# Encoder block on one core: one tile for w_out and feed-forward operands in the place of the normalised input, output tiles split a group ahead, another order of the attention's deferred work

## The chip, the core and the metric

The kernel runs on 1 core of one Trainium2 chip. The metric is the device time in microseconds (us) of one execution. A kernel's figure is the median of several executions. "PE" is the matrix engine, "DVE" the vector engine, "ACT" the scalar engine, "POOL" the general engine and "SP" the engine whose queue issues nearly all DMA transfers. Each engine works through its own list in order. A wait at the head of a list holds up everything behind it.

## What is computed

One block of a transformer encoder for 1024 tokens of width 1024, all in float32. The reference, cut to what matters:

```python
h = layer_norm(x, ln0_g, ln0_b)
proj = h @ w_in + b_in                      # 1024 x (3*512 + 512 + 2*128 + 2*1024)
qa, ka, va, qb, kb, vb, ga, gb = split(proj)
# na: 8 heads, each token sees 8 x 16 neighbours on a 16 x 64 grid, bias rpb
y_na  = neighbourhood_attention(qa, ka, va, rpb) @ w_branch_na
# swa: 8 query heads over 2 key/value heads, |i-j| <= 128, a sink logit
y_swa = windowed_gqa_with_sink(rotary(qb), rotary(kb), vb, sink) @ w_branch_swa
mixed = sigmoid(ga) * y_na + sigmoid(gb) * y_swa
h = layer_norm(2**0.25 * h + mixed @ w_out + b_out, ln1_g, ln1_b)
u = square(relu(h @ w_ff1 + b_ff1))         # 1024 x 4096
return layer_norm(2**0.25 * h + u @ w_ff2 + b_ff2, ln2_g, ln2_b)
```

## The kernel before

**Products.** Float32 factors are split into two fp16 parts, a high and a low one, and three fp16 products stand for one float32 product. A 128x512 piece of result so takes 12 or 24 matmuls of one kind. A split is one ACT instruction (the high part) and one DVE instruction (scaled value minus high part); before it stands a scale, for which ACT sums squares, PE adds the sums over the partitions (a 128x2 matmul on ones), and DVE and POOL finish. The gate products and both feed-forward products use a 2x2 block scheme with fewer products (Winograd's form of Strassen's), whose operands are sums of blocks: A11, A12, A21, A22 and S1 to S4.

**Stages, in the order of time.** First layer norm and the first projections (to 100 us in the trace); attention, while PE fills the gaps with projection matmuls (100 to 400); the rest of the gate products (to 476); the branch products with w_branch and the gates (to 563); w_out with the second layer norm (to 657); the first feed-forward product (657 to 950); the second, with the last layer norm (to the end).

**The order of work is written by hand**: Python code issues the instructions in one sequence, and each engine's list is what falls to it. What matters around the change:

- `steps(s, n)` is one attention step for one pair of query blocks, with n "fill" matmuls (L430), 12 in the steps to 240 us and 18 after. In it, `part_a` issues the scores of step s+2 (L780, L781, two PSUM banks, `ps_s` and `ps_t`). DVE reads them with bias and row maximum (L782), ACT takes the exponentials (L801, L804), `part_l` makes the low part of the probabilities on DVE (L813) and SP transposes them with a DMA into `pt` (L816). `part_c` multiplies by the values (L888, bank `ps_o`, two buffers), and two steps share one bank. ACT takes the upper half out (`evac`, L894), and DVE adds the lower half later (`evac2`, L897), which frees the bank.
- `defer(count, fn, ...)` puts a piece of work off until so many fill matmuls have been issued, and `flush` runs what is due. A step has flushes in the middle and one at its end; only the one at the end runs the pieces that need PE. D_E2 is the count of `evac2`. `norm` (L859) scales the finished chunk by the reciprocals of its sums, which DVE makes (L832, L834), PE transposes (L838, into `ps_t`) and SP brings back through DRAM (L851).
- Other work passes through the same lists: the gathering of projections (ACT L620, L700), the rotary shuffle (DVE L628), the query's high part (ACT L677) and low part (DVE L682), the low halves of weight chunks (DVE L266), and sums for scales (PE L194 into `ps_s`, DVE L200).
- In the branch stage `wo_load`, `wo_square`, `wo_split` prepare the eight 128-row pieces of w_out. The raw rows go through a ring of two buffers "raw"; the split ones lie in `wo`, in the place (pool `r1`) that the normalised input `hT` held until the gate products ended. `between` is work put between the matmuls of a product. `o_hi` and `o_lo` (L1280, L1287) split the attention's output for the branch.
- In the w_out stage, group g is 128 tokens: `split_mx(g)` (L1503, L1504) splits the mixed input, `out_mm(g, half)` (L1628) is 24 matmuls, then `ln1_norm`, `turn` (eight transposes, L1656), `turn_evac` (L1664, L1667) and `combine` (L1673, L1686 to L1690: block sums and their splits). The first feed-forward weights ("head", p = 0 to 3) are prepared here too: `head_w` loads, `squares1` (ACT L1705) and `sum_sq1` (PE L1710), `scale1`, `head_split` (L1719, L1722).
- The first feed-forward product follows (`ff1_mm`, L1795). At its start, A22 is split whole by `comb_hi` (ACT L2025) and `comb_lo` (DVE L2028).

Of the kernel before, what the change touches and what calls it, by code (L numbers as in the profile page):

```python
# [16 lines left out]
P = 128  # L17
D = 1024
# [58 lines left out]
D_E2 = 12  # L77
# [16 lines left out]
def encoder_block(ctx, tc, x, w_in, w_br, w_out, w_ff1, w_ff2, par, rows, rpbp,  # L94
# [10 lines left out]
    r1x, wx = ExitStack(), ExitStack()  # L105
    r1p = r1x.enter_context(tc.tile_pool(name="r1p", bufs=1))
# [330 lines left out]
    def defer(*fns, pe=False, early=False, only=False):  # L437

        later.append([fns[0], fns[1:], pe, early or only, only])
# [414 lines left out]
    def norm(o_chunk):  # L854
        rb = recip.pop(o_chunk)
        sc = na_v[o_chunk][1][:, 1:2] if o_chunk < 4 else swa_sc[0][:, o_chunk // 2 - 2:o_chunk // 2 - 1]
        for x in range(2):
# [4 lines left out]
    def part_c(s):  # L862
# [26 lines left out]
        if t % 2 == 1:  # L889
# [47 lines left out]
    with tc.manual_schedule(engines=MANUAL):  # L937
# [110 lines left out]
        def steps(s, n, before_b=None, before_c=None):  # L1048
# [17 lines left out]
            flush(False)  # L1066
# [5 lines left out]
            flush(False)  # L1072
            pump(part[2])
            flush()
# [318 lines left out]
        def wo_load(k):  # L1393
            raw = wo_raw[k] = wp.tile([P, D], F32, tag="raw", name="raw", bufs=2)
# [39 lines left out]
        for n, (p, i) in enumerate(gseq[2:], 2):  # L1434
# [13 lines left out]
            if n in (4, 5, 6, 7, 10, 11):  # L1448
# [15 lines left out]
        wo = r1p.tile([P, 2, NK, D], F16, tag="r1", name="wo")  # L1464
# [10 lines left out]
        mhl = {}  # L1475
# [23 lines left out]
        def split_mx(g):  # L1499

            m = xps[g % 2].tile([P, 2, 8, P], F16, tag="m", name="m")
# [37 lines left out]
        for f in range(8):  # L1539
            for half in range(2):  # L1540
                if half == 0:
                    wo_split(f)
                    if f + 3 < 8:
# [3 lines left out]
                else:  # L1547
                    if f + 2 < 8:
                        wo_load(f + 2)
                    if f and f + 1 < 8:  # L1550
                        b_split(f + 1)
# [123 lines left out]
    def combine(g):  # L1675
# [15 lines left out]
        split_op("S1", s1, ts_)  # L1691

# [119 lines left out]
    with tc.manual_schedule(engines=MANUAL):  # L1812
# [10 lines left out]
        for g in range(NCG):  # L1823
            out_mm(g, 0, 0, 8)
            if 2 <= g + 1 < NCG:
                split_mx(g + 1)
# [10 lines left out]
            if g == 7:  # L1837
# [4 lines left out]
            if g == 7:  # L1842
                for p in range(2, 4):
                    scale1(p, head_ps[p])
                more_ring(0)
# [7 lines left out]
            if 2 <= g < 4:  # L1853
# [7 lines left out]
            if g == 6:  # L1861
                for p in range(2, 4):
                    squares1(p, raws[p])
# [12 lines left out]
            if g < 2:  # L1876
# [4 lines left out]
            if g == 5:  # L1881
                for p in range(2, 4):
                    head_w(p)
# [63 lines left out]
        r1x.close()  # L1947
        qp = ctx.enter_context(tc.tile_pool(name="qp", bufs=1, reuse_waits="tile"))
        for i, n in enumerate(("S3", "S4", "A22")):
            t = places[n] = qp.tile([P, 8192], F16, tag=f"q{i}", name="h" + n)  # L1950
            ops[n] = t[:, 0:4096].rearrange("p (a k n) -> p a k n", a=2, k=4)
        usl = qp.tile([P, 8, 512], F32, tag="q3", name="usl")
        ufree = [usl[:, i] for i in range(8)]
# [614 lines left out]
```

## Times and profile before

| what | us |
| --- | --- |
| median of 3 executions | 1257.42 (1257.39 to 1257.99) |
| the profiled execution, its own time | 1256.27 |
| its span in the trace | 1254.5 |
| PE busy | 1216.4, 97% of the span |
| DVE busy | 971.1, 77% |
| ACT busy | 868.5, 69% |
| POOL busy | 330.5, 26% |

Read the busy shares first: PE is busy nearly throughout, so the time is its work and the gaps in it. The mean granted clock of PE is 0.994. Which stage holds the gaps, and who ends them, is read in the stretches by stage and in the list of PE's waits, which the prediction shows.

### The profile page before, as it was taken

The page shows a single profiled execution, that of the slowest core. Times are in us where ns is not written, and L with a number is a line of the kernel's source. Part 1 is how long each engine was busy: PE and PEld are TensorE (multiplying, and loading weights), DVE is VectorE, ACT ScalarE, POOL GpSimd, SP SyncE. Part 2 cuts the span into 40 slices and gives each one's busy share as a digit, 9 for nine tenths or more (in the row PEclk, how much of TensorE's full clock was granted, in tenths as well). Part 3 has the DMA queues.
Part 4 walks back from the last instruction along what each step waited for, and adds up shares of the span by engine and source line. Part 5 has one row for each costly group of instructions (what it writes and reads, how often), then busy time and mean ns, then how long its engine had stood idle before and what let it go on. Part 6 is the DMA issues. An engine that isn't in the chain of part 4 may idle for free.

```text
span 1254.5 us, 17213 instructions
## 1 busy us (share of the span) xinstructions
PE 1216.4 (97%) x6070; PEld 607.8 (48%) x6070; DVE 971.1 (77%) x1418; ACT 868.5 (69%) x1415; POOL 330.5 (26%) x368
## 2 busy tenths in 40 slices
PE   7999889999999999999999999999999999999996
PEld 4545556555555444444444444444444444444443
DVE  7687888788787985645678977778857777898888
ACT  6567779998895667853567877787776746344446
POOL 5212220443430003446620013422300002211207
PEclk9999999999999999999999999999999999999998
DMA  8654657767764446636233357766637535363333
GB/s 312 198 183 87 153 127 166 169 170 169 161 162 104 151 151 201 202 101 251 101 151 109 133 191 248 246 234 233 215 108 264 218 135 226 126 260 126 126 109 134
DMA packets 177879, 216.84 MB, mean 173 GB/s; under 512 B 111745, under 2 KB 125313, under 8 KB 171137
## 3 DMA queue, kind: packets, MB, share of 16 engines
q1 hardware_dynamic: 176816, 214.89, 54.0%
q8 instruction: 47, 0.77, 0.3%
q10 hardware_dynamic: 976, 0.87, 0.2%
q14 instruction: 40, 0.32, 0.1%
HBM read 130.69 MB, written 59.33 MB: 151 GB/s over the span
## 4 chain that ended last, share of the span: by engine, by line
PE 71%; DVE 11%; ACT 8%; issue 3%; POOL 3%; DMA 1%; SPq 0%; POOLq 0%; DVEq 0%; ACTq 0%
PE ps_mm L430 13%; PE ps_t L1795 6%; PE ps_o L1795 6%; PE ps_s L2273 6%; PE ps_mm L2273 6%; PE ps_mm L1795 6%; PE ps_t L2273 5%; PE ps_o L2273 5%; PE ps_s L1795 2%; PE ps_o L888 2%; PE ps_o L1176 2%; PE ps_mm L1176 1%; PE ps_t L1176 1%; ACT ss L801 1%; PE ps_o L420 1%
## 5 line engine op out<-in xcount | busy, mean ns | idle before, releaser
L430 PE MATMUL ps_mm<-hT 128*128 128x512 f16 x960 | 227.5, 381 | 5.2 <-DVE hT L399 2.0
L1795 PEld LDWEIGHTS <-tw 128*128 128x128 f16 x1248 | 122.1, 99 | 146.1 <-issue 1.6
L2273 PEld LDWEIGHTS <-hS 128*128 128x128 f16 x1008 | 98.7, 98 | 118.2
L430 PEld LDWEIGHTS <-hT 128*128 128x128 f16 x960 | 90.7, 99 | 103.6 <-issue 14.3
L801 ACT ACTIVATE ss<-ss,sk 128x384 f32<-128x384 f32 (+1 forms) x128 | 73.9, 578 | 32.7 <-DVE sk L782 32.1
L1795 PE MATMUL ps_t<-hS,tw 128*128 128x512 f16 x384 | 88.1, 379 | 1.5 <-ACT sn L1899 1.1
L430 PE MATMUL ps_mm<-hT,wpair 128*128 128x512 f16 x288 | 70.0, 384 | 1.1 <-ACT hT L700 1.1
L1989 DVE TENSOR_TENSOR usl<-usl 128x512 f32<-128x512 f32 x64 | 52.3, 818 | 23.5 <-ACT usl L1917 23.3
L201 POOL TENSOR_TENSOR hT<-hT 128x2 f32<-128x2 f32 x30 | 29.7, 989 | 150.9 <-DVE hT L200 150.9
L1716 POOL TENSOR_TENSOR c<-c 128x2 f32<-128x2 f32 x16 | 15.5, 975 | 195.0 <-DVE c L1715 195.0
L2293 POOL TENSOR_TENSOR acc<-acc,rst 128x512 f32<-128x512 f32 x16 | 31.8, 1987 | 122.5 <-DMA rst<-xr_d 114.6
L2106 DVE SCALAR_TENSOR_TENSOR hS<-stg,c,hS 128x2048 f16<-128x2048 f32 x21 | 49.9, 2378 | 7.7 <-ACT hS L2103 7.7
L888 PE MATMUL ps_o<-pt,vv 128*128 128x256 f16 (+1 forms) x448 | 49.1, 250 | 5.9 <-DMA pt<-pl 3.8
L1722 DVE SCALAR_TENSOR_TENSOR tw<-raw,c,tw 128x512 f16<-128x512 f32 x60 | 51.2, 853 | 4.2 <-ACT tw L1719 3.9
L2273 PEld LDWEIGHTS <-hA 128*128 128x128 f16 x336 | 32.9, 98 | 39.7
L1176 PEld LDWEIGHTS <-hT 128*128 128x128 f16 x336 | 32.8, 99 | 39.6 <-issue 1.1
L813 DVE SCALAR_TENSOR_TENSOR pl<-ss,pl 128x768 f16<-128x768 f32 (+1 forms) x42 | 46.0, 1096 | 2.5 <-ACT pl L804 2.4
L888 PEld LDWEIGHTS <-vv 128*128 128x128 f16 x448 | 35.7, 98 | 23.0 <-issue 6.7
L1795 PE MATMUL ps_o<-hS,tw 128*128 128x512 f16 x192 | 44.0, 379 | 0.0
L1719 ACT ACTIVATE tw<-raw,c 128x512 f16<-128x512 f32 x60 | 41.7, 708 | 2.8 <-DVE raw L1760 2.8
L2273 PE MATMUL ps_mm<-hA,hS 128*128 128x512 f16 x192 | 42.9, 379 | 0.0
L2273 PE MATMUL ps_s<-hA,hS 128*128 128x512 f16 x192 | 42.7, 379 | 0.0
(435 smaller groups left out, 3045.5 us busy)
## 6 DMA issues: line engine op xcount, KB each, us to landing
us_d<-usl SPq DMA_DIRECT2D x112, 256.0 KB, 3.0
stg<-us_d SPq DMA_DIRECT2D x28, 1024.0 KB, 4.8
raw<-in_w_ff SPq DMA_DIRECT2D x24, 512.0 KB, 5.6
sg<-sg_d SPq DMA_DIRECT2D x32, 256.0 KB, 2.9
hA<-in_w_ff SPq DMA_DIRECT2D x8, 1024.0 KB, 7.8
hS<-in_w_ff SPq DMA_DIRECT2D x8, 1024.0 KB, 8.0
hT<-in_w_in SPq DMA_DIRECT2D x60, 128.0 KB, 2.5
hT<-in_w_in SPq DMA_DIRECT2D x11, 512.0 KB, 4.6
```

Of the source, the lines that this page charges most:

```text
L430: PE.matmul(ps, a[:, k, :], act(b, k), start=(k == 0 and i == 0), stop=(k == NK - 1 and i == 2))
L801: ACT.activation(p, p, AF.Exp, bias=nm[:, i:i + 1], scale=-1.0, accum_out=sums_l[o_chunk][:, hh, 2 * t + i:2 * t + i + 1])
L813: DVE.scalar_tensor_tensor(out=pl[:, n:2 * n], in0=e[:, 0:n], scalar=P_SCALE, in1=pl[:, 0:n], op0=ALU.mult, op1=ALU.subtract)
L888: PE.matmul(o, vs, move(part), start=(m == 0 and part == 0), stop=(m == len(runs) - 1 and part == 1))
L1176: PE.matmul(ps, w[:, a, k, :], act[:, b, k, :], start=(first and k == 0 and m == 0), stop=(k == 3 and m == 2), skip_group_check=True)
L1719: ACT.activation(hi_lo(slot, 0), src, AF.Copy, bias=0.0, scale=w_scale(p))
L1722: DVE.scalar_tensor_tensor(out=hi_lo(slot, 1), in0=src, scalar=w_scale(p), in1=hi_lo(slot, 0), op0=ALU.mult, op1=ALU.subtract)
L1795: PE.matmul(ps, ww, act[:, part, k, :], start=(first and k == 0 and m == 0), stop=(k == 3 and m == 2), skip_group_check=True)
L1989: DVE.tensor_tensor(out=out, in0=a, in1=b, op=op)
L2106: DVE.scalar_tensor_tensor(out=slot[:, :, 1, :], in0=src, scalar=scale, in1=slot[:, :, 0, :], op0=ALU.mult, op1=ALU.subtract)
L2273: PE.matmul(ps, st[:, a, part, j * P:(j + 1) * P], w[:, a, wpart, :], start=(first and a == 0 and m == 0), stop=(a == 3 and m == 2), skip_ ...
L2293: POOL.tensor_tensor(out=z, in0=z, in1=t, op=ALU.add)
```

## The change

- **Attention.** D_E2 goes from 12 to 14. `norm` is deferred by itself, in two halves (counts D_E2+2 and D_E2+8), and runs only in the flush in the middle of a step (`mid=True`). The flush at the end of a step is gone; the one behind `part_c` now runs everything, PE's pieces too. As the counts fall due at other flushes, DVE's `evac2`, shuffle, query low part and the reciprocals change place against L782 and L813.
- **One tile `r1w`** takes the place of the normalised input: the first half is `wo`, the second holds the raw rows of w_out from k = 2 on (which no longer share the ring of two). Later, A22, the raw weights of the heads p = 2 and 3, S3 and S4 lie in it; `usl`, the partial results of the first feed-forward product, moves to the second halves of S1 and S2.
- **Branch.** `wo_load(f+2)` is issued in the first half of f rather than the second; `o_lo(5)` comes after the last gate product; `between` (two sums for scales on PE) goes from behind the first product to the middle of the second.
- **w_out stage.** `split_mx(g+2)` at group g in place of g+1. `head_w(2)` and `(3)` at groups 2 and 3 (were at 5), their `squares1` at 4 and 5 (were both at 6), their sums and scales at 6 (were at 7). `combine` from group 4 on also splits its part of A22, and `comb_hi`, `comb_lo` of A22 go.
- **Start of the first feed-forward product.** `ff1_mm(1, 2)` and the work behind two earlier products come before `turn(7)`.

PE has the same instructions in number before and after.

```diff
-D_E2 = 12
+D_E2 = 14
...
-    def flush(pe=True, early=False):
+    def flush(pe=True, early=False, mid=False):
         for e in list(later):
-            if e[0] <= 0 and (pe or not e[2]) and (e[3] or not early) and (early or not e[4] or not in_steps):
+            if e[0] <= 0 and (pe or not e[2]) and (e[3] or not early) and (early or not e[4] or not in_steps) \
+                    and (mid or not e[5] or not in_steps):
...
                 if t == 3 and o_row == 64:
-                    defer(D_E2, evac2, 2, lambda: norm(o_chunk))
+                    defer(D_E2, evac2)
+                    for x in range(2):
+                        defer(D_E2 + 2 + 6 * x, lambda x=x: norm(o_chunk, x), mid=True)
...
-            flush(False)
+            flush(False, mid=True)
             pump(part[1])
             if before_c:
                 before_c()
             if s >= C_LAG:
                 part_c(s - C_LAG)
-            flush(False)
+            flush()
             pump(part[2])
-            flush()
...
-            raw = wo_raw[k] = wp.tile([P, D], F32, tag="raw", name="raw", bufs=2)
+            raw = wo_raw[k] = wp.tile([P, D], F32, tag="raw", name="raw", bufs=2) if k < 2 else wo_rest[:, k]
...
                 o_hi(n_o)
-                if n < 10:
+                if n < 7:
                     o_lo(n_o)
                 n_o += 1
-        o_lo(6)
-        o_lo(7)
+        for c in (5, 6, 7):
+            o_lo(c)
...
-        wo = r1p.tile([P, 2, NK, D], F16, tag="r1", name="wo")
+        r1w = r1p.tile([P, 4, NK, S], F16, tag="r1", name="r1w")
+        wo = r1w[:, 0:2]
+        wo_rest = r1w[:, 2:4].rearrange("p a k s -> p (a k s)").bitcast(F32).rearrange("p (k n) -> p k n", n=D)
...
-            m = xps[g % 2].tile([P, 2, 8, P], F16, tag="m", name="m")
+            if g < 2:
+                xm.append(xps[g].tile([P, 2, 2, 8, P], F16, tag="m", name="m"))
+            m = xm[g % 2][:, g // 2 % 2]
...
-                gemm3(ps, bws[f], lambda part, k: act(part, k, half), nk=4, k0=4 * gi)
-                if gi == 0 and between:
+                n = 2 if gi and between else 4
+                gemm3(ps, bws[f], lambda part, k: act(part, k, half), nk=n, k0=4 * gi, last=(n == 4))
+                if n == 2:
                     between()
+                    gemm3(ps, bws[f], lambda part, k: act(part, k + 2, half), nk=2, k0=6, first=False)
...
                     wo_split(f)
+                    if f + 2 < 8:
+                        wo_load(f + 2)
...
+    qs = [r1w[:, i].rearrange("p k s -> p (k s)") for i in range(4)]
+    q3 = [qs[3][:, 4096 * i:4096 * (i + 1)].bitcast(F32) for i in range(2)]
+    for i in range(2):
+        raws[2 + i] = q3[i].rearrange("p (r c k n) -> p r c k n", r=2, c=2, k=4)
+    q_place(2, "A22")
...
+        split_op("A22", a22, ts_)
...
-            if 2 <= g + 1 < NCG:
-                split_mx(g + 1)
+            if g + 2 < NCG:
+                split_mx(g + 2)
...
-            if g == 7:
+            if g == 6:
                 head_ps += [sum_sq1(p, "o") for p in range(2, 4)]
...
-            if 2 <= g < 4:
+            if 2 <= g < 6:
                 squares1(g - 2, raws[g - 2])
...
-            if g == 6:
-                for p in range(2, 4):
-                    squares1(p, raws[p])
...
-            if g < 2:
+            if g < 4:
                 head_w(g)
...
-        usl = qp.tile([P, 8, 512], F32, tag="q3", name="usl")
+        usl = [places[n][:, 4096:8192].bitcast(F32).rearrange("p (a n) -> p a n", a=4) for n in ("S1", "S2")]
...
         ff1_mm(1, 1)
+        after1(0, 1)
+        after1(0, 2)
+        ff1_mm(1, 2)
         turn(7)
         turn_evac(7)
         more_ring(1)
-        after1(0, 1)
-        after1(0, 2)
-        ff1_mm(1, 2)
         combine(7)
...
-            if n == 0:
-                comb_hi("A22")
-            elif n == 1:
-                comb_lo("A22")
-            elif n == 2:
+            if n == 2:
                 more_tw()
```

**How the lists move.** In the changed kernel the line numbers are one higher from the attention on, and some 17 higher in the w_out stage. The first place is DVE's list in the attention, at 129 to 140 us of the trace of before; L782 (L783 in the changed kernel) reads scores, `wpair` is the low half of a weight chunk, `q` the query's low part, `oT` the `evac2`. Before:

```order
L813 SCALAR_TENSOR_TENSOR pl<-ss,pl 128x640
L897 TENSOR_TENSOR oT<-ps_o,oT 64x512
L628 STREAM_SHUFFLE qs<-qf 128x512
L682 TENSOR_TENSOR q<-qf,q 64x4x16x8 x2
L782 ISA ss,sk<-ps_s,bd,snk 128x384
L782 ISA sk 128x1
L782 ISA ss,sk<-ps_t,bd,snk 128x384
L782 ISA sk 128x1
L266 SCALAR_TENSOR_TENSOR wpair<-hT,wpair 128x1024
L813 SCALAR_TENSOR_TENSOR hT<-ss,hT 128x768
```

And the changed kernel, from the same reading of scores on:

```order
L783 ISA ss,sk<-ps_s,bd,snk 128x384
L783 ISA sk 128x1
L783 ISA ss,sk<-ps_t,bd,snk 128x384
L783 ISA sk 128x1
L266 SCALAR_TENSOR_TENSOR wpair<-hT,wpair 128x1024
L814 SCALAR_TENSOR_TENSOR hT<-ss,hT 128x768
L898 TENSOR_TENSOR oT<-ps_o,oT 64x512
L629 STREAM_SHUFFLE qs<-qf 128x512
L783 ISA ss,sk<-ps_s,bd,snk 128x384
L783 ISA sk 128x1
L783 ISA ss,sk<-ps_t,bd,snk 128x256
L783 ISA sk 128x1
L814 SCALAR_TENSOR_TENSOR pl<-ss,pl 128x768
L683 TENSOR_TENSOR q<-qf,q 64x4x16x8 x2
```

`evac2` and the shuffle now stand behind the reading of the next scores and its L814, and the two query low parts one reading later still; before, all stood ahead of it. The second place is SP's list at the start of the branch stage (`sg` are gate rows, `braw` the raw rows of w_branch). Before:

```order
L1512 DMA sg<-sg_d 128x512 x6
L1373 DMA braw<-in_w_br 128x1024
L1512 DMA sg<-sg_d 128x512 x2
L1395 DMA raw<-in_w_out 128x1024
```

And the changed kernel:

```order
L1518 DMA sg<-sg_d 128x512 x6
L1397 DMA r1w<-in_w_out 128x1024
L1375 DMA braw<-in_w_br 128x1024
L1518 DMA sg<-sg_d 128x512 x4
```

The raw rows of w_out are now ahead of the raw rows of w_branch and of two gate rows. The third place is ACT's list in the w_out stage, around group 6 (`junk` is the sum of squares, `hS` and `hA` and `r1w` operands, `tw` weights). Before:

```order
L285 ACTIVATE z<-z,mv 128x1024
L1705 ACTIVATE junk,c_5477<-hS_6064 128x2048
L1705 ACTIVATE junk,c_5477<-hS_6065 128x2048
L1672 CAST hS_6065<-s2t 128x4x128
L1672 CAST hS_6064<-s1t 128x4x128
L1719 ACTIVATE tw_5476<-hA_5475,c_5477 128x512 x2
L1667 ACTIVATE mx<-ps_t,c_5477 128x128 x6
```

And the changed kernel:

```order
L285 ACTIVATE z<-z,mv 128x1024
L1688 CAST hS_6060<-s2t 128x4x128
L1688 CAST hS_6059<-s1t 128x4x128
L1688 CAST r1w<-mx 128x4x128
L1736 ACTIVATE tw_5470<-hA_5469,c_5471 128x512 x2
L1683 ACTIVATE mx<-ps_t,c_5471 128x128 x6
```

The two sums of squares of 128x2048 are gone from here (they stand one in each of the two groups before), and a cast of A22's part has come.

More of the change, by code (lines that the diff above doesn't have):

```diff
@@ L435, in encoder_block, with defer @@
     later = []
-    def defer(*fns, pe=False, early=False, only=False):
-        later.append([fns[0], fns[1:], pe, early or only, only])
-    def flush(pe=True, early=False):
+    def defer(*fns, pe=False, early=False, only=False, mid=False):
+        later.append([fns[0], fns[1:], pe, early or only, only, mid])
+    def flush(pe=True, early=False, mid=False):
         for e in list(later):
-            if e[0] <= 0 and (pe or not e[2]) and (e[3] or not early) and (early or not e[4] or not in_steps):
+            if e[0] <= 0 and (pe or not e[2]) and (e[3] or not early) and (early or not e[4] or not in_steps) \
+                    and (mid or not e[5] or not in_steps):
                 later.remove(e)
@@ L852, in load_recip, with norm @@
                               rl_d[o_chunk, hh * 8:(hh + 1) * 8, :].rearrange("a b -> (a b)").partition_broadcast(64))
-    def norm(o_chunk):
-        rb = recip.pop(o_chunk)
+    def norm(o_chunk, *xs):
+        rb = recip[o_chunk]
         sc = na_v[o_chunk][1][:, 1:2] if o_chunk < 4 else swa_sc[0][:, o_chunk // 2 - 2:o_chunk // 2 - 1]
-        for x in range(2):
+        for x in xs or range(2):
             z = oT[:, o_chunk, x * 512:(x + 1) * 512]
@@ L1546, in encoder_block @@
                         b_scale(f + 1)
[L1547 to L1551, printed above, removed]
+                elif f and f + 1 < 8:
+                    b_split(f + 1)
                 g, h = (f, 1) if half == 0 else (f + 1, 0)
@@ L1596, in encoder_block, with q_place @@
     op_places("A11", "A12")
+    qs = [r1w[:, i].rearrange("p k s -> p (k s)") for i in range(4)]
+    q3 = [qs[3][:, 4096 * i:4096 * (i + 1)].bitcast(F32) for i in range(2)]
+    for i in range(2):
+        raws[2 + i] = q3[i].rearrange("p (r c k n) -> p r c k n", r=2, c=2, k=4)
+    def q_place(i, n):
+        places[n] = qs[i]
+        ops[n] = qs[i][:, 0:4096].rearrange("p (a k n) -> p a k n", a=2, k=4)
+    q_place(2, "A22")
     tw3 = hp.tile([P, 4, 2, 512], F16, tag="t3", name="tw3")
@@ L1841, in encoder_block @@
                 head_ps = [sum_sq1(p, "o") for p in range(2)]
-            if g == 7:
+            if g == 6:
                 for p in range(2, 4):
                     scale1(p, head_ps[p])
+            if g == 7:
                 more_ring(0)
@@ L1880, in encoder_block @@
                     scale1(p, head_ps[p])
-            if g == 5:
-                for p in range(2, 4):
-                    head_w(p)
             if g == 6:
@@ L1946, in after1 @@
                 act_fn(p, 0, "A21", a, None, 0)
[L1947 to L1951, printed above, removed]
-        usl = qp.tile([P, 8, 512], F32, tag="q3", name="usl")
-        ufree = [usl[:, i] for i in range(8)]
+        for i, n in enumerate(("S3", "S4")):
+            q_place(i, n)
+        usl = [places[n][:, 4096:8192].bitcast(F32).rearrange("p (a n) -> p a n", a=4) for n in ("S1", "S2")]
+        ufree = [u[:, i] for u in usl for i in range(4)]
         ff1_mm(0, 1)
@@ L2181, in second @@
         def second(n):
-            return places[n][:, 4096:8192].bitcast(F32)
+            return q3["S1 S2".split().index(n)] if n in ("S1", "S2") else places[n][:, 4096:8192].bitcast(F32)
         def turn_over(i):
@@ L2442, in encoder_block @@
                 if n == 1 and j == 1:
-                    t = qp.tile([P, 2, 4, 512], F32, tag="q3", name="w2c")
-                    wring[0:0] = [t[:, x] for x in range(2)]
+                    wring[0:0] = usl
                     nc.sync.dma_start(xts[0][:, 0, :], row_bc(0))
```

10 lines of the change are left out of this document (5 added, 5 removed).

## The prediction

> **What bounds the kernel now.** I began with the stretches by stage, to see where PE has gaps. Columns: stretch, its length, then busy time (and instructions) of PE, PE's weight load, DVE, ACT and POOL, then the granted clock, DMA share and GB/s.
>
> ```profile
> 100.00:240.00 140.00, 128.06 (x742) 76.45 (x740) 111.59 (x231) 114.63 (x243) 38.90 (x53) 0.98 0.63 143
> 140.00:150.00 10.00, 7.60 (x38) 4.42 (x38) 8.90 (x16) 7.34 (x17) 2.82 (x4) 0.83 0.56 142
> 180.00:190.00 10.00, 8.48 (x44) 5.31 (x44) 8.89 (x19) 7.34 (x16) 1.42 (x3) 0.83 0.65 176
> 240.00:400.00 160.00, 160.00 (x919) 93.11 (x918) 131.47 (x266) 136.58 (x267) 49.89 (x65) 1.00 0.68 158
> 625.00:700.00 75.00, 69.04 (x333) 32.72 (x332) 62.37 (x95) 53.69 (x90) 13.51 (x15) 1.00 0.32 114
> 700.00:1215.00 515.00, 514.99 (x2409) 235.96 (x2408) 408.35 (x443) 334.45 (x444) 92.86 (x64) 1.00 0.55 193
> ```
>
> PE is without a gap in 240 to 400 and 700 to 1215, so nothing can be won there. It lacks 140.00 - 128.06 = 11.9 us in the first half of the attention and 75.00 - 69.04 = 6.0 us around the second layer norm. In 140:150 and 180:190 the clock is 0.83, which costs 10 x 0.17 = 1.7 us each, 3.4 together. 515 us over 2409 matmuls gives 0.214 us for one.
>
> The lists of PE's waits say who ends the gaps: total, times, longest. First 100 to 240 us.
>
> ```profile
> PE ps_o L888 <- DMA pt<-pl: 3.8, 2, 3.1
> PE ps_t L838 <- DVE sk L782: 2.2, 1, 2.2
> PE ps_mm L430 <- ACT hT L700: 2.2, 2, 1.1
> PE ps_o L888 <- DMA pt<-hT: 2.1, 1, 2.1
> PE ps_s L194 <- DVE sk L782: 1.6, 2, 1.3
> ```
>
> They add up to the 11.9. Next the branch stage (465 to 563; 2.3 in all), then 625 to 700 us (5.9).
>
> ```profile
> PE ps_mm L1176 <- DVE go L1251: 0.8, 1, 0.8
> PE ps_t L422 <- DVE wb L1391: 0.7, 1, 0.7
> PE ps_s L1491 <- DVE prm L1485: 0.6, 1, 0.6
> PE ps_s L1402 <- ACT bc L1398: 0.2, 1, 0.2
> ```
>
> ```profile
> PE ps_t L1656 <- ACT z L285: 2.0, 2, 1.6
> PE ps_o L1710 <- ACT junk L1705: 1.7, 1, 1.7
> PE ps_t L1795 <- ACT sn L1899: 1.1, 1, 1.1
> PE ps_mm L1628 <- DVE m L1504: 0.5, 1, 0.5
> PE ps_t L1795 <- DVE tw L1722: 0.4, 1, 0.4
> PE ps_s L1795 <- DVE usl L1919: 0.3, 1, 0.3
> ```
>
> PE's own work is the same before and after, so the change is worth what it takes from these 20.1 us and the 3.4 of the clock, less what it adds.
>
> **Attention.** The worst gaps have one cause, followed back in the timelines (start, duration, instruction, idle time before it and who ended it) of PE, DVE and ACT.
>
> ```profile
> 130.51 0.34 PE L781 MATMUL ps_t<-kl,q 128*128 128x384 f32 x1
> 134.31 0.28 PE L781 MATMUL ps_t<-kl,q 128*128 128x256 f32 x1
> 143.42 0.82 PE L888 MATMUL ps_o<-pt,vv 128*128 128x256 f16 x8 [2.10 <-DMA pt<-hT]
> ```
>
> ```profile
> 119.37 0.01 DVE L628 LOAD_MASK_SELECT qs<-qf  x1 [2.45 <-ACT qf L620]
> ...
> 130.58 0.68 DVE L897 TENSOR_TENSOR oT<-ps_o,oT 64x512 f32<-64x512 f32 x1
> ...
> 135.27 0.69 DVE L682 TENSOR_TENSOR q<-qf,q 64x512 fp32r<-64x512 f32 x1 [2.52 <-ACT q L677]
> 135.99 0.62 DVE L782 CUSTOM_DVE_ANT_0 ss<-ps_s,bd,snk 128x384 f32<-128x384 f32 x1
> ...
> 137.07 2.11 DVE L266 SCALAR_TENSOR_TENSOR wpair<-hT,wpair 128x1024 f16<-128x1024 f32 x1
> 139.11 0.94 DVE L813 SCALAR_TENSOR_TENSOR hT<-ss,hT 128x768 f16<-128x768 f32 x1
> ```
>
> ```profile
> 134.63 0.61 ACT L677 CAST q<-qf 64x512 fp32r<-64x512 f32 x1 [2.60 <-PE ps_t L781]
> ```
>
> The scores were done at 130.85, but DVE read them (L782) at 135.99: it stood 2.52 us at the query's low part (L682), which waits for ACT's high part, and this for PE's scores at 134.31, the last readers of the old query. L813 so ended at 140.05, and the transposed probabilities came to PE at 143.42, 3.4 us later. In the changed list L682 and the shuffle stand behind this L813. Then L782 starts at 130.9, L266 at 131.9 and L813 at 134.0, ending at 134.9, and the probabilities arrive by 138.3. PE would want them at 143.42 less the two gaps (2.1 and 1.1), so 140.2. Both gaps go. The pair around 180 us (3.1 and 1.1) has the same shape and goes with it, the 1.3 of L194 too, and L838's 2.2, whose DVE stood 2.45 us at the shuffle (119.37): of that I keep 0.8, as the reciprocals now stand behind one more L813. With both pairs the clock spells should go. Gross: 2.1 + 1.1 + 3.1 + 1.1 + 1.3 + 2.2 + 3.4 = 14.3, less 0.8 = 13.5.
>
> What it adds: `evac2` (L897) now follows the next L782, L266 and L813, and until it ends, the bank for the pair after next isn't free. From the scores that is (137.07 - 135.99) + (139.11 - 137.07) + 0.94 + 0.68 = 4.7 us. PE needs the bank one step (134.31 - 130.51 = 3.8) and eight fill matmuls (1.7) later, 5.5: a margin of 0.8. It doesn't hold where L813 is slow:
>
> ```profile
> 125.77 1.78 DVE L813 SCALAR_TENSOR_TENSOR pl<-ss,pl 128x640 f16<-128x640 f32 x1
> ...
> 188.43 0.82 DVE L813 SCALAR_TENSOR_TENSOR pl<-ss,pl 128x640 f16<-128x640 f32 x1
> ```
>
> ```profile
> 125.59 1.28 POOL L632 TENSOR_TENSOR qs<-qs,rt 128x512 f32<-128x512 f32 x1
> ```
>
> The same shape takes 1.78 while POOL runs and 0.82 otherwise, 0.96 more than a margin of 0.8. Some 8 places have the L266 in between. Bounds: 0, and 8 x 1.78 = 14.2. I take 0.5 at each, 4.0, nearer to the lower end, since the fast form leaves room. Behind a waiting L888 stand four fill matmuls and the next scores, so such a wait is paid in full. Net 9.5 (-0.7 to 13.5).
>
> The Trainium skill (SBUF — State Buffer, "Who interferes with whom") says that a DVE instruction with two SBUF inputs contends for a shared port with a GpSimd instruction that reads SBUF; the pair of L813 above agrees. By it, a new order pays wherever it lays L813 on POOL's rotary sums. It also says (TensorE: Matmul & The Clock Gate, "HAM oscillation — how this bites in real kernels") that only idle stretches over about 3.4 us bring the slow clock. The trace differs: the clock is 0.83 where the gaps were 1.1 and 2.1. By the page the two spells would come from something else and stay, and the sum below would be 11.6 in place of 15.0; by the trace it is 15.0, and a pair of waits left over costs 1.7 more.
>
> On SP the two loads of the reciprocals (L851) now stand behind one more transpose; PE doesn't read them, and `norm`, which does, is itself put off by 2 to 8 fill matmuls more. If they came late, `norm` would stop DVE ahead of the next L782, which is the stop described above, at the end of each of the eight chunks; I cost it at nothing, as the half-chunk `norm` in the middle flush stands behind that step's L813.
>
> In the steps after 240 us there is no gap to win and, with 18 fill matmuls, 6 x 0.214 = 1.3 us more room for the new order. I cost it at nothing; without that room it would be the 0.5 a pair of above.
>
> **Branch.** Two rows of ACT and DVE:
>
> ```profile
> 493.89 1.06 ACT L1398 ACTIVATE bc<-raw 128x1024 fp8e5<-128x1024 f32 x1 [1.81 <-DMA raw<-in_w_out]
> ```
>
> ```profile
> 468.37 1.22 DVE L1287 TENSOR_TENSOR oS<-oT,oS 128x1024 f16<-128x1024 f32 x1
> ```
>
> ACT waits 1.81 us for raw rows of w_out, and the 0.2 and 0.7 of PE come from ACT's list behind it. The rows are now asked for half a product pair earlier (12 matmuls or more, 2.6 us) and wait for no buffer: both go. The 0.8 goes as `o_lo(5)` (1.22) leaves the place before L1251. The 0.6 goes as `between` moves six matmuls (1.3) later. The added load order holds back two gate rows and one w_branch piece on SP, one transfer each; they were not waited for on PE. Of 2.3 I take 1.9 (0 to 2.3).
>
> **Second layer norm and start of the feed-forward.**
>
> ```profile
> 650.12 1.90 ACT L1705 ACTIVATE junk<-hS 128x2048 fp8e5<-128x2048 f32 x1
> ...
> 678.84 1.88 ACT L2025 CAST hS<-mx 128x2048 f16<-128x2048 f32 x1
> ```
>
> ```profile
> 654.69 0.69 DVE L1673 TENSOR_TENSOR hS<-s2t,hS 128x512 f16<-128x512 f32 x1 [5.15 <-ACT hS L1672]
> ...
> 686.18 2.29 DVE L2028 TENSOR_TENSOR hS<-mx,hS 128x2048 f16<-128x2048 f32 x1
> ```
>
> The two sums of squares (1.9 each) leave ACT's place ahead of the casts for which DVE stood 5.15 us; with them goes the 1.7 of L1710. The 1.6 of L1656 has 12 matmuls (2.6) of cover more and goes. The 1.1 goes because A22's 1.88 on ACT and 2.29 on DVE are done in quarters in the groups before (four times 0.69 on DVE, somewhat less on ACT), in time that DVE stood idle. The 0.3 goes with them. The 0.5 goes too, but comes back one group later at L1656, since the chain from `z` to the transposes is no shorter. The 0.4 of L1722 grows to about 1.2: PE comes there 4.1 us earlier (1.7 + 1.6 + 0.5 + 0.3), DVE only 5.15 - 1.9 = 3.3. Left are 0.4 + 0.5 + 1.2 = 2.1, more with A22's pieces in the way: I take 2.3 left of 5.9, 3.6 won (1.5 to 5.5). The head loads p = 2 and 3, moved two and three groups ahead, and `usl` and A22 in other places of the same memory wait for `wo` and S1, S2, which are read last before those are due; the DMA share of 0.32 in 625:700 leaves the loads room. Were one of them late, `squares1` would wait on ACT, and the 1.7 would stay.
>
> Sum: 9.5 + 1.9 + 3.6 = 15.0. Against the profiled execution, 1256.27 - 15.0 = 1241.3; the median stood 1257.42 - 1256.27 = 1.15 above it, so 1242.4.
>
> **The rivals.**
> - *DVE becomes the bound of the attention.* For it: 111.59 of 140 busy, and 8.90 of 10 in 140:150; once PE doesn't wait, the same DVE work falls into some 126 us, 89%, and each collision with POOL adds 0.96. Against it: DVE's own stops (2.45, 2.52) go as well. The attention then gains nothing, the rest 5.5: 1251.9, from 1248 to 1254.9.
> - *All gaps go and no new one comes.* For it: the fast L813 leaves 0.8 at each bank. 13.5 + 1.9 + 3.6 = 19.0 gives 1238.4, with all of the 2.3 and 5.9 another 2.7 less: about 1237, from 1235.7 to 1238.4.
> - *The change moves the waits, and the total stays*: the work of each engine is the same, and each removed stop returns at the next product. For it: the 0.5 does just this. Against it: L813 is followed to a margin of 140.2 - 138.3 = 1.9. About 1257.
> - *Slower: the late `evac2` holds the bank `ps_o` at every pair.* The first half has 16 pairs of steps. If each waits the 1.78 of a slow L813, 28.5 us stand against 19.0 won: 1257.42 + 9.5 = 1266.9. It is slower from 12 pairs on (21.4). Against it: only about half the steps have the L266 ahead, and POOL is busy only 38.90 of 140 us.
>
> **How the numbers follow.** Forecast (1238.4 to 1248) 0.55; DVE the bound 0.20; all gaps gone 0.10; no change 0.06; slower 0.09. A measurement of this kernel tells about 0.2% (2.5 us) from no change, so faster means under 1254.9: 0.55 + 0.20 + 0.10 = 0.85; same 0.06, slower 0.09. For 8 in 10 the range takes the forecast's own, most of the full gain and three quarters of the DVE case: 1235.5 to 1252.5.
>
> **What would show it.** Right: in 100 to 240 us PE's waits at L888 for `pt` fall to the 0.7 that stands there beside the 3.1, the clock is 1.00 in both spells, L682 has no long stop ahead of L782, and small waits at L888 on DVE's `oT` appear. In 465 to 563 almost nothing is left; at the start of the feed-forward some 2 us, at L1656 and on `tw`. Wrong: waits at L888 on `oT` of over 1 us in most pairs, DVE without idle time while PE waits for `pt`, or gaps in 240 to 400.

## The result, and the profile after

The changed kernel takes 1238.08 us (median of 4, 1237.36 to 1239.03), the kernel before 1257.7 on the same chip: a ratio of 0.9843, with a 95% interval of 0.9826 to 0.986. It is 19.6 us faster. The forecast was 1242.4, with a range of 1235.5 to 1252.5. The profiled executions took 1256.27 us (before) and 1237.68 (after), with spans of 1254.5 and 1235.7.

The stretches by stage of the kernel after (columns as in the prediction; the work in a stretch of clock time came later before, by up to 12 us in the attention and by up to 18 from 625 us on):

```profile
100.00:240.00 140.00, 135.86 (x810) 81.73 (x808) 122.02 (x252) 123.18 (x261) 42.95 (x55) 1.00 0.68 156
240.00:400.00 160.00, 159.62 (x922) 92.07 (x920) 129.75 (x258) 135.11 (x258) 51.81 (x66) 1.00 0.68 159
625.00:700.00 75.00, 72.73 (x348) 34.34 (x349) 65.08 (x103) 56.88 (x103) 4.10 (x6) 1.00 0.30 102
700.00:1215.00 515.00, 515.00 (x2409) 236.10 (x2408) 410.36 (x439) 333.75 (x447) 103.50 (x76) 1.00 0.53 189
```

PE's idle time in 100 to 240 us falls from 11.9 to 4.1 us, although DVE is now busy for 122.0 of 140 us rather than 111.6, and the clock there is 1.00. PE's waits in the kernel after, for 100 to 240 us, then 465 to 563, then 625 to 700:

```profile
PE ps_s L194 <- DVE sk L783: 1.9, 3, 0.8
PE ps_o L889 <- DMA pt<-hT: 1.5, 1, 1.5
PE ps_o L889 <- DVE oT L898: 0.7, 1, 0.7
```

```profile
PE ps_mm L1637 <- ACT m L1509: 0.9, 1, 0.9
```

```profile
PE ps_t L1672 <- ACT z L285: 1.6, 1, 1.6
PE ps_s L1812 <- DVE hS L1931: 1.3, 1, 1.3
PE ps_t L1812 <- DVE tw L1739: 0.3, 1, 0.3
```

The six waits of over 1 us in the attention are gone, and so are all four of the branch stage. New are 1.5 and 0.7 at L889, 0.9 at the first w_out product, 1.3 at L1812, and 0.4 at L430 near 361 us, in a stretch that had no gap before. The 1.6 at the transposes (L1672) is in the sixth group, where before 0.4 stood; the 1.6 of before was in the last.

To see what each stage is worth, I measure from one PE instruction to another that stands at the same place in both kernels. In PE's timeline of before these are the first scores, the first gate product, the first transposes of the second layer norm, and the last sum for a scale in the first feed-forward product:

```profile
88.92 0.47 PE L780 MATMUL ps_s<-kh,q 128*128 128x256 f32 x1
...
400.14 2.11 PE L1176 MATMUL ps_mm<-hT 128*128 128x512 f16 x9
...
581.63 1.04 PE L1656 MATMUL ps_t<-ident,z 128*128 128x128 f32 x8
...
915.19 0.28 PE L1710 MATMUL ps_s<-c 128*128 128x2 f32 x2
```

And after:

```profile
88.61 0.47 PE L781 MATMUL ps_s<-kh,q 128*128 128x256 f32 x1
...
387.78 1.46 PE L1178 MATMUL ps_mm<-hT 128*128 128x512 f16 x6
...
567.11 1.04 PE L1672 MATMUL ps_t<-ident,z 128*128 128x128 f32 x8
...
896.78 0.28 PE L1727 MATMUL ps_s<-c 128*128 128x2 f32 x2
```

| stage, us | before | after | gain | forecast |
| --- | --- | --- | --- | --- |
| attention (scores to gate products) | 311.22 | 299.17 | 12.05 | 9.5 |
| gates and branch (to the transposes) | 181.49 | 179.33 | 2.16 | 1.9 |
| w_out and first feed-forward | 333.56 | 329.67 | 3.89 | 3.6 |

The rest of the span's 18.8 us, 0.7, lies ahead of the scores and in the last 340 us. Each row rests on one trace of each kernel. How far such a length varies is seen in those kernels below whose order of work in a stage is the changed one's: the attention takes 298.3 to 300.3 us in eight traces, the w_out stage 329.65 to 329.82 in five that have no slow clock there. So the 12.05 is known to about 1 us, and the 3.89 more closely.

### The profile page after: what moved, and what is told of

Its sections match the earlier page's. It is cut to its first block, busy times and chain, and to the rows that moved or that the text cites. A ratio compares the mean times of both kernels' runs of the same rounds, so it can differ in the third digit from the quotient of the medians.

```text
span 1235.7 us, 17241 instructions
## 1 busy us (share of the span) xinstructions
PE 1210.1 (98%) x6070; PEld 606.1 (49%) x6070; DVE 976.1 (79%) x1421; ACT 867.3 (70%) x1418; POOL 333.9 (27%) x368
## 4 chain that ended last, share of the span: by engine, by line
PE 78%; DVE 8%; ACT 6%; issue 2%; POOL 2%; DMA 1%; SPq 0%; POOLq 0%; ACTq 0%; DVEq 0%
PE ps_mm L430 14%; PE ps_t L1812 6%; PE ps_o L1812 6%; PE ps_mm L1812 6%; PE ps_mm L2278 6%; PE ps_s L2278 6%; PE ps_t L2278 5%; PE ps_o L2278 5%; PE ps_s L1812 3%; PE ps_o L889 2%; PE ps_o L1178 2%; PE ps_mm L1178 1%; PE ps_t L1178 1%; PE ps_t L420 1%; PE ps_t L421 1%
## 5 line engine op out<-in xcount | busy, mean ns | idle before, releaser
L430 PE MATMUL ps_mm<-hT 128*128 128x512 f16 x960 | 226.4, 380 | 4.5 <-DVE hT L399 2.0
L1812 PEld LDWEIGHTS <-tw 128*128 128x128 f16 x1248 | 122.1, 99 | 145.0 <-DVE tw L1739 0.8
L2278 PEld LDWEIGHTS <-r1w 128*128 128x128 f16 x1008 | 98.7, 98 | 118.4
L430 PEld LDWEIGHTS <-hT 128*128 128x128 f16 x960 | 90.7, 99 | 102.0 <-issue 12.0
L430 PE MATMUL ps_mm<-hT,wpair 128*128 128x512 f16 x288 | 68.8, 380 | 0.0
L201 POOL TENSOR_TENSOR hT<-hT 128x2 f32<-128x2 f32 x30 | 25.6, 852 | 114.1 <-DVE hT L200 114.1
L2112 ACT ACTIVATE hA<-r1w,c 128x2048 f16<-128x2048 f32 x10 | 20.0, 1996 | 50.0 <-DVE r1w L2167 26.8
L2115 DVE SCALAR_TENSOR_TENSOR r1w<-stg,c,r1w 128x2048 f16<-128x2048 f32 x21 | 49.6, 2360 | 4.0 <-ACT r1w L2112 4.0
L2278 PEld LDWEIGHTS <-hS 128*128 128x128 f16 x336 | 32.9, 98 | 39.4
L889 PE MATMUL ps_o<-pt,vv 128*128 128x256 f16 (+1 forms) x448 | 49.2, 250 | 2.2 <-DMA pt<-hT 1.5
L814 DVE SCALAR_TENSOR_TENSOR pl<-ss,pl 128x768 f16<-128x768 f32 (+1 forms) x42 | 46.3, 1101 | 2.2 <-ACT pl L805 2.0
L1998 DVE TENSOR_TENSOR hS<-hS,hS 128x512 f32<-128x512 f32 x41 | 33.6, 820 | 14.6 <-ACT hS L1929 14.5
L889 PEld LDWEIGHTS <-vv 128*128 128x128 f16 x448 | 35.5, 98 | 19.3 <-DVE oT L898 1.9
L1812 PE MATMUL ps_t<-hS,tw 128*128 128x512 f16 x192 | 44.1, 379 | 0.3 <-DVE tw L1739 0.3
L1812 PE MATMUL ps_t<-r1w,tw 128*128 128x512 f16 x192 | 44.0, 379 | 0.0
L1812 PE MATMUL ps_o<-r1w,tw 128*128 128x512 f16 x192 | 44.0, 379 | 0.0
```

The costliest lines, as they stand in the source:

```text
L430: PE.matmul(ps, a[:, k, :], act(b, k), start=(k == 0 and i == 0), stop=(k == NK - 1 and i == 2))
L814: DVE.scalar_tensor_tensor(out=pl[:, n:2 * n], in0=e[:, 0:n], scalar=P_SCALE, in1=pl[:, 0:n], op0=ALU.mult, op1=ALU.subtract)
L889: PE.matmul(o, vs, move(part), start=(m == 0 and part == 0), stop=(m == len(runs) - 1 and part == 1))
L1812: PE.matmul(ps, ww, act[:, part, k, :], start=(first and k == 0 and m == 0), stop=(k == 3 and m == 2), skip_group_check=True)
L1998: DVE.tensor_tensor(out=out, in0=a, in1=b, op=op)
L2115: DVE.scalar_tensor_tensor(out=slot[:, :, 1, :], in0=src, scalar=scale, in1=slot[:, :, 0, :], op0=ALU.mult, op1=ALU.subtract)
```

## The experiments

Each kernel was timed beside the kernel before on its own chip. "Stage" below is the length between the same PE instructions as in the table, from the kernel's own trace.

**The attention's order.** Two kernels split the change in two.

```diff
 # att_undone: the changed kernel with
-D_E2 = 14
+D_E2 = 12
-                    defer(D_E2, evac2)
-                    for x in range(2):
-                        defer(D_E2 + 2 + 6 * x, lambda x=x: norm(o_chunk, x), mid=True)
+                    defer(D_E2, evac2, 2, lambda: norm(o_chunk))
-            flush(False, mid=True)
+            flush(False)
 ...
-            flush()
+            flush(False)
             pump(part[2])
+            flush()
 # att_alone: the kernel before with the reverse of this
```

> The changed kernel with the attention's part undone (D_E2 12, evac2 and norm together, the flush at the end of a step back); storage, branch and w_out stage as changed. Theory: the attention's order is worth the 12.1 us by which the traces part there (101 to 406 us), and nothing after it depends on it: 1238.1 + 12.1 = 1250.2, with the waits of before at L888 (2.1 and 3.1) and a clock of 0.83 in two stretches of 10 us. Rival (storage helps the attention too): under 1246.

> The kernel before with the attention's part of the change alone. Theory: 1257.7 - 12.1 = 1245.6, and the small waits left in 100 to 240 us are those of the changed kernel (1.5 and 0.7 at L889, 1.9 at L194). Rival (parts not additive, a wait of the attention's order returns in the gate products): over 1249.

Measured: undone, 1251.8 us (ratio 0.9944, 0.9929 to 0.9959); alone, 1244.31 (0.9889, 0.9873 to 0.9906). The product of the two ratios is 0.9834, the whole change 0.9843: the parts add up. The stage of the attention is 312.88 us without its part and 298.53 with it alone. The theory holds: the attention's gain comes without the new storage and the later stages, and goes with them in place.

**What in it does the work.** Two more kernels undo one half each.

```diff
 # de2_12: the changed kernel with
-D_E2 = 14
+D_E2 = 12
 # endflush: the changed kernel with
-            flush()
+            flush(False)
             pump(part[2])
+            flush()
```

> The changed kernel with D_E2 back at 12 and all else as changed, so that evac2 stands ahead of the reading of the scores again, but query low part and shuffle keep their new places. Theory (DVE's stop at the query's low part and the shuffle was the cause, evac2's place is not): within 2 us of the changed kernel, 1236.5 to 1240, with evac2 ending over 1 us before its bank is wanted. Rival (evac2 ahead of the scores' reading was the delay): 1242 or more, with waits at L889 for pt.

> The changed kernel with the flush for PE's pieces moved back to the end of a step (the one behind part_c runs only the others, as before), D_E2 still 14 and norm in halves. Theory: this flush is what sets shuffle and query low part ahead of or behind L783, so most of the attention's 12.1 us is lost: 1246 to 1252, with DVE idle for 2 us and more at L683 ahead of L783. Rival (D_E2 and the halves of norm carry the gain): under 1241.

With the flush at the end of the step back, the kernel takes 1249.07 us (0.9923, 0.9908 to 0.9937), 11 more than the changed one, and the stage is 310.33. DVE's and ACT's timelines of that kernel show the old stop:

```profile
136.81 0.69 DVE L683 TENSOR_TENSOR q<-qf,q 64x512 fp32r<-64x512 f32 x1 [4.15 <-ACT q L678]
137.53 0.62 DVE L783 CUSTOM_DVE_ANT_0 ss<-ps_s,bd,snk 128x384 f32<-128x384 f32 x1
```

```profile
136.17 0.61 ACT L678 CAST q<-qf 64x512 fp32r<-64x512 f32 x1 [4.22 <-PE ps_t L782]
```

DVE stands 4.15 us at the query's low part, and L783 behind it reads scores that were done by 132.4 us. The flush moves every piece that is due, not the query's work alone; that the stop at L683 is what costs is read from these rows. So the cause is the place of the query work ahead of the scores' reading, and one flush decides it.

With D_E2 at 12 the kernel takes 1236.24 us (0.9825, 0.981 to 0.984), 1.8 less than the changed one at the medians; its stage is 296.48, 2.7 shorter than in the trace of the changed kernel and 1.8 to 3.8 shorter than in the eight traces of that order. Its waits in 100 to 240 us:

```profile
PE ps_o L889 <- DMA pt<-hT: 1.6, 1, 1.6
PE ps_s L194 <- DVE sk L783: 0.7, 1, 0.7
```

Two of the three waits at L194 and the one for `oT` are gone. `norm`, whose counts this edit moves too, keeps its place in DVE's list (behind the same L814, near 140 and 172 us). So the later `evac2` isn't part of the gain; it costs some 2 to 3 us of it. Two rows of the changed kernel, of DVE and of PE, show how near it runs:

```profile
140.35 0.68 DVE L898 TENSOR_TENSOR oT<-ps_o,oT 64x512 f32<-64x512 f32 x1
```

```profile
141.09 0.83 PE L889 MATMUL ps_o<-pt,vv 128*128 128x256 f16 x8
```

`evac2` frees the bank at 141.03, and PE starts to fill one at 141.09.

**The w_out stage, one edit at a time.**

```diff
 # split_g1
-            if g + 2 < NCG:
-                split_mx(g + 2)
+            if 2 <= g + 1 < NCG:
+                split_mx(g + 1)
 # a22_whole: no split_op("A22") in combine; at the first two feed-forward products
+            if n == 0:
+                comb_hi("A22")
+            elif n == 1:
+                comb_lo("A22")
 # squares_late: squares1(2) and (3) at group 6, their sums and scales at group 7
 # ff1_order
+        turn(7)
+        turn_evac(7)
+        more_ring(1)
         after1(0, 1)
         after1(0, 2)
         ff1_mm(1, 2)
-        turn(7)
-        turn_evac(7)
-        more_ring(1)
```

> The changed kernel with the output tiles split one group ahead of their use again in the program (at group g the split of g+1, as before). Theory: the 0.5 us that PE waited for the split at group 5 returns and the 1.6 us at the transposes of group 5 (L1672) falls by as much or more, since the chain on DVE from L1510 over L1651 to L1655 ends when it ends: within 0.5 us of the changed kernel. Rival (splitting ahead is worth the 0.5 and the idle that goes with it): 0.7 us slower than the changed kernel.

> The changed kernel with A22 split whole at the start of the first feed-forward product, as before (1.9 us on ACT, 2.3 on DVE), and not in quarters in combine. Prediction's step: PE's 1.1 us at L1812 behind ACT's sn return, 1.1 to 1.3 slower. Rival from the trace after: the last two quarters stand on DVE (0.69 each) right ahead of L1931, for which PE now waits 1.3 us; without them that falls to about 0.6, and the whole nets 0.4 to 0.6 slower. If both are hidden: no difference.

> The changed kernel with the sums of squares of the heads p = 2 and 3 both at group 6 again and their sums and scales at group 7, as before. Theory: they stand on ACT (1.9 each) ahead of the casts of group 5 and PE waits 1.7 us at L1727 again: 1.7 to 2 us slower than the changed kernel, 1239.8 to 1240.2. Rival (the wait at L1672 of group 6 or 7 takes it over, hidden now): no difference.

> The changed kernel with ff1_mm(1, 2) and the work behind the two products before it standing behind the last transposes again, as before. Theory: the last transposes lose 12 matmuls (2.6 us) of cover and PE waits there 1.6 us or more (before: 1.6), while the 1.3 at L1812 behind DVE's L1931 falls: net 0.5 to 2 us slower. Rival (the wait only changes its place): no difference within 0.3.

| kernel | median, us | ratio to before (95%) | stage | against after |
| --- | --- | --- | --- | --- |
| changed | 1238.08 | 0.9843 (0.9826 to 0.986) | 329.67 | |
| split_g1 | 1238.46 | 0.9847 (0.9832 to 0.9862) | 331.00 | +1.3 |
| a22_whole | 1237.25 | 0.9841 (0.9826 to 0.9856) | 331.09 | +1.4, of it 1.7 clock |
| squares_late | 1241.72 | 0.9875 (0.9858 to 0.9891) | 333.52 | +3.9 |
| ff1_order | 1237.97 | 0.9843 (0.9828 to 0.9857) | 329.51 | -0.2 |

The sums of squares are worth 3.9 us of stage and 3.6 of the median, twice what was expected. Their waits from 563 to 720 us:

```profile
PE ps_s L1812 <- DVE hS L1933: 4.0, 2, 2.7
PE ps_t L1672 <- ACT z L285: 1.6, 1, 1.6
PE ps_o L1727 <- ACT junk L1722: 1.1, 1, 1.1
```

The wait for the sum itself is only 1.1. The larger part is that DVE, kept from its casts for 5 us, is still late when it comes to L1933 (L1931 in the changed kernel) in the feed-forward product: 4.0 us in two waits in place of 1.3 in one. DVE's rows of this kernel:

```profile
640.17 0.69 DVE L1689 TENSOR_TENSOR hS<-s2t,hS 128x512 f16<-128x512 f32 x1 [5.15 <-ACT hS L1688]
...
658.42 0.74 DVE L1933 SCALAR_TENSOR_TENSOR hS<-ps_s,c,sn 128x512 f32<-128x512 f32 x1
```

In the changed kernel these two stand at 635.80 and 653.94, and the stop at the first is 1.22.

A22 in quarters is worth nothing. The waits with A22 whole, from 563 to 720 us:

```profile
PE ps_t L1672 <- ACT z L285: 1.6, 1, 1.6
PE ps_t L1811 <- ACT sn L1910: 1.1, 1, 1.1
PE ps_t L1811 <- DVE tw L1738: 0.4, 1, 0.4
```

The 1.1 behind `sn` is back, but the 1.3 at L1931 is gone: one has taken the other's place. The order at the start of the feed-forward product is worth nothing here either: the last transposes don't wait without it, and the waits at L1931 add up to 1.2, where they are 1.3 with it. But each edit was undone with the others in place. With the squares late and the new order kept, the last transposes don't wait either, where the kernel before, with both old, had 1.6. So squares and order may cover for each other there, and undoing them singly can't show what the order would be worth alone. Splitting a group ahead is worth 1.3 us of stage in this pair of traces. The medians, 0.4 apart on different chips, don't separate the two, so this one is shown by the traces alone. At the sixth group it gains nothing: without it PE waits 0.5 for the split and 0.4 at the transposes, with it 1.6 at the transposes. The gain is at L1812 behind L1931: 1.3 in one wait, where without the split ahead there are 2.6 in two. The single gains, 3.9 and 1.3, come to more than the stage's 3.89, so they don't simply add up.

**The branch stage.**

```diff
 # branch_back
-                if n < 7:
+                if n < 10:
                     o_lo(n_o)
 ...
 # wo_load(f + 2) in the second half of each f, and the sums of scales
 # between the two products again
-                n = 2 if gi and between else 4
+                n = 4
 ...
+                if gi == 0 and between:
+                    between()
```

> The changed kernel with three edits of the branch stage undone together, told apart by place in the trace: the fifth low part of the attention's output back between the gate products; w_out's raw rows asked for in the second half of each f again (still in the new tile); the two sums for scales back between the two products. Theory: the 0.8 at the gate products and the 0.2 + 0.7 of the scale's sum and of w_branch return; 0.6 returns at the sum for the mixed input's scale, and the 0.9 at the first w_out product goes. In all 1.2 to 1.8 slower than the changed kernel, 1239.3 to 1239.9. Rival (the new tile itself, without the ring of two, is what let the rows come in time): the 0.2 and 0.7 stay away, 0.5 slower.

Measured: 1239.44 us (0.9847, 0.9827 to 0.9868), as expected; the stage from the gate products to the transposes is 181.10 us, 1.8 longer than in the changed kernel. Its waits from 450 to 563 us are those of before but for the 0.2, and the 0.9 at the first w_out product is gone:

```profile
PE ps_mm L1178 <- DVE go L1253: 0.8, 1, 0.8
PE ps_t L422 <- DVE wb L1393: 0.7, 1, 0.7
PE ps_s L1495 <- DVE prm L1489: 0.5, 1, 0.5
```

The 0.8 and the 0.7 are back with the edits that took them, so the new tile alone isn't what let the raw rows come in time; the 0.2 stayed away. The move of `between` did not do what it was costed at: the mixed input's scale comes six matmuls later, six fewer stand between it and the first w_out product, and 0.5 before the sum becomes 0.9 after it.

**Towards a better kernel.** Two attempts on what was left.

```diff
 # late_early: the changed kernel with
-D_NA = 4
+D_NA = 6
-D_E2 = 14
+D_E2 = 12
-        LATE = {0: (2,), 1: (3, 4), 2: (5,), 3: (6,), 4: (7,)}
+        LATE = {0: (2,), 1: (3, 4), 2: (5, 6), 3: (7,)}
 # best2: this and
-        defer(4, scale, 4, high, 5, low, 8, turn)
+        defer(4, scale, 4, high, 5, low, 18, turn)
 # squares1 of group 5 behind head_split(0, 1) and (0, 2); the last quarter of A22
 # split at the first product of the feed-forward's loop
```

> An attempt to better the changed kernel. D_E2 is 12; D_NA goes from 4 to 6, which puts the key low parts (L570, L571) behind the next reading of scores, as the change did with the query's; and POOL's additions for the late residual rows (L1825) are all done by group 3 of the w_out stage, a group earlier. Theory: the 1.6 us at L889 near 209 us goes for the reason of the 2.1 and 3.1 before; DVE's split at group 5 (L1689 x2 2.99, L1510 2.15) runs without POOL beside it in some 1.4 and 1.3, 2.5 us less, so the 1.6 at the transposes of group 5 goes. 1236.2 less 1.6, 1.6 and the refill of PE after each (0.2): 1232.5 to 1234. Rival (POOL's own order then holds back the norm of group 2 or 3, or the chain waits elsewhere): 1235.5 or more.

> The attempt taken further: D_E2 12, D_NA 6 and POOL's late rows early as in the attempt before, and three more edits. The value transposes (L492) stand ten fill matmuls later, so behind the transposed probabilities on SP, which at 206 us issues them 2.3 us after DVE has made them; theory: the 1.9 us at L889 near 210 us goes. At group 5 of the w_out stage the sum of squares (1.9 on ACT) stands behind the casts of the head weights, for which DVE waited 1.3 us; theory: the 1.2 at the transposes goes. The last quarter of A22 is split two products later, behind L1931; theory: the 1.3 at L1812 falls to some 0.6. 1234.9 - 1.9 - 1.2 - 0.7 - 0.2 each for two refills of PE = 1230.7; 1230 to 1232.5. Rival (each chain has another member right behind, and the wait changes its name): 1233.5 or more.

> The changed kernel itself once more, on the same chip as the attempt, as its measure: 1237 to 1239, 0.2% or more above the attempt. If its 1.6 us at the transposes of group 5 (L1672) is again there, the execution shows whether the clock falls behind it: by the executions so far in two of nine.

The first took 1234.91 us (0.9814, 0.9795 to 0.9832). Both halves of its theory fell short. The two parts of DVE's split at group 5 took 1.3 each, as expected, but DVE then waited 1.3 for ACT's head weights, behind a sum of squares, and the 1.6 at the transposes only fell to 1.2. And the wait near 209 us stayed, at 1.9. DVE had made the probabilities in time, but SP issued their transpose late, behind two value transposes (L492) and three loads, as DVE's and SP's rows of that kernel show:

```profile
198.56 0.82 DVE L814 SCALAR_TENSOR_TENSOR hT<-ss,hT 128x640 f16<-128x640 f32 x1
```

```profile
204.24 1.58 SPq L817 DMA_TRANSPOSE pt<-hT  x1
```

They were ready at 199.4 and asked for at 204.2. The second attempt moves L492 behind them, beside its two edits in the w_out stage. It takes 1231.51 us (0.9793, 0.9779 to 0.9808), within what was expected; the changed kernel on the same chip takes 1237.51 (0.9842, 0.9825 to 0.9858). So it is 6.0 us faster than the changed kernel and 25.8 faster than the one before; its edits were not undone singly. All its waits from 95 to 720 us:

```profile
PE ps_mm L1637 <- ACT m L1509: 0.9, 1, 0.9
PE ps_mm L430 <- ACT vf L504: 0.8, 1, 0.8
PE ps_s L1813 <- DVE hS L1933: 0.7, 1, 0.7
PE ps_s L194 <- DVE sk L783: 0.6, 1, 0.6
PE ps_t L1813 <- DVE tw L1740: 0.4, 1, 0.4
```

## Why the prediction was right, step by step

- **The sum: what it counted came, and 3 us that it did not count came too.** Over the three stages PE's idle time fell by 11.6 us (7.4, 1.4 and 2.8; in the attention from 11.94 of 311.22 us to 4.52 of 299.17) and the slow clock gave 3.4: together 15.0, the forecast. That this sum fits is luck: the attention gave 1.3 more of it than forecast, the other two stages 1.3 less. The traces gained 18.1. The other 3.0 (1.2, 0.8 and 1.0) is time in which PE is listed as busy. So the step "PE's own work is the same before and after, so the change is worth what it takes from these 20.1 us and the 3.4 of the clock" was too narrow: its instructions are the same, its busy time isn't. Branch and w_out stage came near their forecasts only with this time, since idle time gave 1.4 of the 1.9 and 2.8 of the 3.6.
- **Attention, the cause: right.** The stop at the query's low part was the delay, as the kernel with the old flush shows. Without the later `evac2` the stage is 14.7 us shorter (311.22 - 296.48), where the gross was put at 13.5.
- **Attention, the charge: right in kind, too large.** The step "I take 0.5 at each, 4.0" measured 2.7 (299.17 - 296.48) in this pair of traces. Only 0.7 of it is a wait for the bank. Another 1.2 is at L194, where PE waits for L783, which stands behind the same `evac2`; the step looked at the bank alone. What is left, some 0.8 on balance, is small waits elsewhere and busy time. This charge and the gross make about equal parts of the distance from 9.5 to 12.05. The 0.8 left at L838 didn't come. The sign "PE's waits at L888 for `pt` fall to the 0.7" was missed: 1.5 stands there near 211 us, which the attempts traced to SP's order.
- **Branch: right in sum, one step wrong.** "The 0.6 goes as `between` moves six matmuls (1.3) later" counted what hides the sum and not what waits for it: the split of the first output tile is behind it, and lost the same six matmuls. 0.9 came for 0.6. The 0.2 and 0.7 went, as the kernel that asks late for the raw rows shows for the 0.7.
- **w_out stage: 3.6 against 3.89, but by another way.** Two steps gave gains to edits that show none when undone alone: "The 1.6 of L1656 has 12 matmuls (2.6) of cover more and goes" (it stays away without them) and "The 1.1 goes because A22's 1.88 on ACT and 2.29 on DVE are done in quarters" (the quarters put 1.3 elsewhere, at the wait whose 0.3 was to vanish). The squares are worth the most, 3.9, since they free DVE's chain for everything behind; the step gave them the 1.7 of L1710 alone. Splitting ahead, counted as nothing on balance, is worth 1.3 in the traces. "Comes back one group later" is right in kind: 1.6 in place of the 0.9 expected. The 0.4 of L1722 is 0.3, not 1.2.
- **The rivals.** DVE isn't the bound: 87% busy in 100 to 240 us, and the kernel with D_E2 at 12 fits more into them yet. The late `evac2` does hold the bank, but at one pair, not twelve (by that rival's own sum eleven, 19.6, are already more than the 19.0 won).

## What to carry to other kernels

On an engine that works in order, an instruction that waits for another engine belongs behind the work whose input is ready, and one flush in the wrong place can cost 11 us of 1250. When work moves later, ask both what hides it now and what waits for it: `between` and `evac2` each paid at the second. When several edits share a gain, undo them singly: here one of four carried most of it. Two that cover the same wait can each look worthless that way, so check such a pair together.

## What the runs showed of the hardware

**A slow stretch of the clock can follow a short wait.** Up to 1215 us, each of the eight slow stretches that the traces show loses 1.70 to 1.71 us (the missing clock summed over windows of 1 us). Inside, the granted clock is 0.50 (the windows from 145 to 148 us of the kernel before), so a stretch lasts 3.4 us. It follows waits far shorter than that. In 13 places, over eleven profiled executions, PE waited once for 1.58 to 1.65 us in the second layer norm; a slow stretch came after two of them. It came after two of eight lone waits of 1.8 to 2.7 us, after four of the six pairs in the attention (1.1 us and 2.1 to 3.1, within 5 us), and nowhere after a lone wait under 1.5 us. What decides which wait it follows isn't shown. The kernel with A22 whole and the changed kernel, one window after the same 1.6 us wait:

```profile
620.00:630.00 10.00, 8.40 (x39) 4.04 (x38) 8.38 (x17) 4.37 (x9) 2.03 (x4) 0.85 0.29 103
```

```profile
620.00:630.00 10.00, 8.37 (x46) 4.33 (x44) 8.57 (x18) 4.88 (x10) 1.22 (x2) 1.00 0.29 107
```

With 39 matmuls and 46 in the same 10 us, the same wait costs 1.7 more in one of them. The Trainium skill (TensorE: Matmul & The Clock Gate, "What's actually happening") gives a free-running window of 3413 ns, and the length of the stretch agrees. The Trainium skill's rule of thumb of no idle gaps over about 3.4 us (TensorE: Matmul & The Clock Gate, "HAM oscillation — how this bites in real kernels") is too loose here: slow stretches followed lone waits of 1.6 us. That it depends on where in such a window the wait falls is a guess that no run tests. Fewer waits so also mean fewer slow stretches. In the last comparison the kernel before ran at mean clocks of 0.992 to 0.996 (7 executions), the changed one at 0.997 to 0.998 (4).

**A wait costs more than its length.** In PE's timeline of before:

```profile
559.61 0.38 PE L422 MATMUL ps_t<-oS,wb 128*128 128x512 f16 x1
560.54 0.38 PE L1491 MATMUL ps_s<-prm,bc 128*128 128x2 f32 x2 [0.55 <-DVE prm L1485]
```

Between the starts lie 0.93 us, where 0.21 is usual: 0.7 is lost for a wait listed as 0.55. The list counts from the end of the matmul of 0.38 ahead, with which the next one would otherwise overlap. So this wait cost 0.17 beside its listed length. Over the three stages there are 9 waits fewer after than before (19 and 10), which at 0.17 each would make half of the 3.0 us by which PE's busy time fell beyond the clock. That is an estimate from one wait; what makes the other half is open.

**The issuing queue can be the wait.** In the first attempt SP took 3.3 us to issue two value transposes, and the finished probabilities stood 4.9 us behind them and the loads; PE's list named only the DMA.
